# Layer 0's key and value evacuation: key low parts written by VectorE into the other partition half, values split in one operation per engine

## The chip, the cores and the metric

One core of a Trainium2 chip runs the whole program in one launch. The metric is the device time of one execution in microseconds (us). The engines are named as in the profile: PE (TensorE matmul), PEld (its weight load), DVE (VectorE), ACT (ScalarE), POOL (GpSimd) and SP (SyncE, which issues nearly all DMAs here; its queue is SPq).

## The reference, cut to what matters

The input is 512 tokens of 1024 features in float32. Layer 0 normalises x, multiplies by one wide matrix (`even_w_in`) and runs two groups of 16 attention heads of 64 channels on the result: forgetting attention ("F") and a mixture of dilated windows ("D"). Each has a gate path; the gated outputs go through `even_w_out` and are added to x. Layer 1 is a retention layer, which the change does not touch, and a last normalisation follows.

```python
def even_layer(x, g_norm, w_in, b_f, w_out):
    z = rms_norm(x, g_norm) @ w_in
    qa, ka, va, ga, fa, qb, kb, vb, gb = jnp.split(z, cuts, axis=-1)
    ...
    ya = forgetting_attention(hA(qa), hA(ka), hA(va), log_f).reshape(Bsz, S, WIDTH_FOX)
    yb = dilated_attention(hB(qb), hB(kb), hB(vb)).reshape(Bsz, S, WIDTH_DIL)
    y = jnp.concatenate([ya * jax.nn.silu(ga), yb * jax.nn.silu(gb)], axis=-1)
    return x + y @ w_out
```

## The kernel before

**Numbers as a sum of two.** Matmul operands are `F32R` values, which keep less of a float32 than it has. So each operand x is held as a high part, written by ACT as a copy into an `F32R` tile, and a low part, written by DVE as x minus the high part. The helper `split` (lines 138 to 144) does one such pair: ACT at L140, DVE at L142. A projection makes three matmuls per pair of operands (`three`, L199 to L201). All the split operations of the kernel have these two lines, so one tells them apart by the tile names: `w_h` and `w_l` are weights, `ka` and `kl` keys, `v` values, `pth` and `ptl` transposed probabilities, `yh` and `yl` gated outputs.

**Groups of heads.** Layer 0's 32 heads are worked in 8 groups of four heads (`ORDER = "DFFFFDDD"`). Each group has four projections of 256 columns: values (`proj_tokens`, result `pt`), keys and queries (`proj_features`, results `pf`, two blocks b of 128 channels, that is two heads each), and the gate. When the last matmul of a block is issued, its `done` function evacuates the PSUM bank: `evac_v`, `evac_k`, `evac_q`, `evac_gate`.

**Keys.** The score matmul of one head contracts over 128 rows: 64 channels of the key's high part and 64 of its low part in one tile, against a query tile arranged in the same way (L491, L492). So of one block, head 0 needs tile `ka` = [high of channels 0 to 63; low of channels 0 to 63] and head 1 needs `kb` = [low of channels 64 to 127; high of channels 64 to 127]. Before, `evac_k` split the whole block into `ka` (high) and a scratch tile `kl` (low), and three DMAs on the sync queue moved halves to the other partitions. `kl` has a single buffer, so the DVE subtraction of the second block waits until the first block's two transfers out of `kl` have landed. There are 16 key blocks: 8 groups of two.

**Values.** `evac_v` gets a bank with two token tiles of four heads of 64 channels. For an even head the value tile holds [high, low], for an odd head [low, high], side by side in 128 columns. Before, the even heads were split by one pair of operations and the odd heads by another, each of 256 elements a partition. There are 16 such banks too.

**The order of the work.** `interleave` runs the attention steps of one group and fills between them with the matmuls of the next group's projections and the output projection, by an estimated share of PE time. A step issues the scores of one head (`softmax_block`: scores, DVE maximum `pi` at L495, ACT exponential at L497, DVE reciprocal at L498, POOL scaling at L499), the transposes of the head before it (`transpose_block`, L506, split into `pth` and `ptl`) and its product with the values (`pv_block`, L518 with `pth`, L519 with `ptl`). `finish_head` adds the two halves of a finished head (`tmp` by ACT at L532, `y` by DVE at L533, both 64 partitions by 512), and every second head POOL multiplies the gate and a split makes `yh` and `yl`. Each engine runs its instructions in one order. Outside of a few marked sections that order is drawn up from the program's dependencies by a scheduler when the program is built.

**Buffers.** Projection results share three PSUM banks (tag `p`). Raw weights (`raw`), `wh` and `wl` have three buffers each. Key tiles have six buffers. Weights are loaded by SP (L164), and a load waits until the raw buffer three loads back has been split. SP's queue is in order: key transfers (L445 to L447), query transfers (L457 to L461), weight loads and the forget-gate rows (L545) stand in one line.

Of the kernel before, what the change touches and what calls it, by code (L numbers as in the profile page):

```python
# [9 lines left out]
F32R = mybir.dt.float32r  # L10
AF = mybir.ActivationFunctionType
ALU = mybir.AluOpType
PSUM = bass.MemoryType.PSUM

P = 128
S = 512
# [43 lines left out]
def trunk(ctx: ExitStack, tc, x, even_norm, even_w_in, even_b_f, even_w_out,  # L60
          odd_norm, odd_w_in, odd_w_out, final_norm, ident_d, dil_d, causal_d, rot_d, dec_d, out):
    nc = tc.nc
    pe, act, dve, pool = nc.tensor, nc.scalar, nc.vector, nc.gpsimd
    dma = nc.sync.dma_start
# [10 lines left out]
    def r32(ap):  # L75
        return ap.bitcast(F32)
# [61 lines left out]
    def split(hi, lo, src, scale=1.0):  # L138

        act.activation(hi, src, AF.Copy, scale=scale)  # L140
        if scale == 1.0:
            dve.tensor_tensor(lo, src, r32(hi), ALU.subtract)  # L142
        else:
            dve.scalar_tensor_tensor(lo, src, scale, r32(hi), ALU.mult, ALU.subtract)
# [206 lines left out]
    with ExitStack() as l0:  # L351
        cst = l0.enter_context(tc.tile_pool(name="cst0", bufs=1))
        qp = l0.enter_context(tc.tile_pool(name="qp", bufs=5))
# [83 lines left out]

        def evac_k(store):
            def done(b, ps):
                ka = qp.tile([P, S], F32R, tag="k", name="ka", bufs=6)  # L440
                kb = qp.tile([P, S], F32R, tag="k", name="kb", bufs=6)
                kl = qp.tile([P, S], F32R, tag="kl", name="kl", bufs=1)
                split(ka, kl, ps)

                dma(out=r32(kb[64:128, :]), in_=r32(kl[64:128, :]))  # L445
                dma(out=r32(kb[0:64, :]), in_=r32(ka[64:128, :]))
                dma(out=r32(ka[64:128, :]), in_=r32(kl[0:64, :]))  # L447
                store.extend([ka, kb])
            return done

# [14 lines left out]
        def evac_v(store):  # L465
            def done(b, ps):
                if b == 0:
                    store.append(gp.tile([P, NT, 4, P], F32R, tag="v", name="v"))
                src = ps.rearrange("p t (h d) -> p t h d", d=64)
                vv = store[0][:, 2 * b:2 * b + 2]  # L470

                split(vv[:, :, 0::2, 0:64], vv[:, :, 0::2, 64:128], src[:, :, 0::2, :])
                split(vv[:, :, 1::2, 64:128], vv[:, :, 1::2, 0:64], src[:, :, 1::2, :])
            return done

        def evac_gate(store):
# [388 lines left out]
```

## Time and profile before

| | |
|---|---|
| median of 3 runs | 1024.42 us (1022.52 to 1027.31) |
| the profiled execution's own time | 1027.15 us |
| its span | 1025.4 us |
| granted TensorE clock | 0.994 of full speed |
| PE busy | 995.8 us, 97% of the span |
| PEld busy | 841.4 us, 82% |
| DVE busy | 630.5 us, 61% |
| ACT busy | 473.6 us, 46% |
| POOL busy | 238.4 us, 23% |
| DMA | 106.82 MB, HBM read 84.87 MB |

The busy time of PE counts overlapping matmuls with a modelled end, so a gap of PE is best read from the start of one matmul to the start of the next. In rows of the timeline the first number is the start in us from the start of the span and the second the duration; brackets at the end give the idle time of that engine before the row and what ended it.

### The profile page before, as it was taken

The page shows a single profiled execution, that of the slowest core. Times are in us where ns is not written, and L with a number is a line of the kernel's source. Part 1 is how long each engine was busy: PE and PEld are TensorE (multiplying, and loading weights), DVE is VectorE, ACT ScalarE, POOL GpSimd, SP SyncE. Part 2 cuts the span into 40 slices and gives each one's busy share as a digit, 9 for nine tenths or more (in the row PEclk, how much of TensorE's full clock was granted, in tenths as well). Part 3 has the DMA queues.
Part 4 walks back from the last instruction along what each step waited for, and adds up shares of the span by engine and source line. Part 5 has one row for each costly group of instructions (what it writes and reads, how often), then busy time and mean ns, then how long its engine had stood idle before and what let it go on. Part 6 is the DMA issues. An engine that isn't in the chain of part 4 may idle for free.

```text
span 1025.4 us, 14433 instructions
## 1 busy us (share of the span) xinstructions
PE 995.8 (97%) x5170; PEld 841.4 (82%) x5170; DVE 630.5 (61%) x1382; ACT 473.6 (46%) x987; POOL 238.4 (23%) x340
## 2 busy tenths in 40 slices
PE   8999999999999999999999989999999999999997
PEld 6878888888887987988988769877888888888875
DVE  6365676575574675675657684377635844683476
ACT  6355464554544644645657464333323332333333
POOL 1011444444344442211212140023100300030012
PEclk9999999999999999999999999999999999999999
DMA  7664777645656775437444126222222232322112
GB/s 204 135 136 88 167 90 117 158 96 121 142 98 118 126 88 139 103 81 156 72 126 123 42 62 205 83 81 83 69 76 82 82 103 61 93 87 89 62 42 83
DMA packets 77130, 106.82 MB, mean 104 GB/s; under 512 B 6001, under 2 KB 49265, under 8 KB 76930
## 3 DMA queue, kind: packets, MB, share of 16 engines
q1 hardware_dynamic: 77058, 105.90, 43.8%
q8 instruction: 41, 0.67, 0.3%
q14 instruction: 31, 0.25, 0.1%
HBM read 84.87 MB, written 2.13 MB: 85 GB/s over the span
## 4 chain that ended last, share of the span: by engine, by line
PE 79%; DVE 8%; DMA 6%; ACT 4%; issue 2%; POOL 1%; SPq 0%; DVEq 0%; POOLq 0%; ACTq 0%
PE pf L199 10%; PE pf L200 10%; PE pf L201 10%; PE pw L201 5%; PE pw L200 5%; PE pw L199 5%; PE po L199 5%; PE po L201 4%; PE po L200 4%; PE pt L201 3%; PE pt L199 3%; PE pt L200 3%; PE ps_pt L506 3%; DVE w_l L142 2%; DMA kb<-ka 2%; PE ps_o L519 2%
## 5 line engine op out<-in xcount | busy, mean ns | idle before, releaser
L142 DVE TENSOR_TENSOR w_l<-w_raw,w_h 128x512 fp32r<-128x512 f32 x288 | 215.0, 773 | 103.0 <-ACT w_h L140 89.1
L140 ACT ACTIVATE w_h<-w_raw 128x512 fp32r<-128x512 f32 x288 | 169.7, 628 | 194.6 <-PE pf L200 61.8
L199 PE MATMUL pf<-xT,w_h 128*128 128x512 f32 x512 | 202.0, 394 | 0.0
L201 PE MATMUL pf<-xT,w_l 128*128 128x512 f32 x512 | 200.9, 392 | 0.0
L200 PE MATMUL pf<-xT,w_h 128*128 128x512 f32 x512 | 200.8, 392 | 0.0
L499 POOL TENSOR_SCALAR pi<-pi,st 128x512 f32<-128x512 f32 (+3 forms) x128 | 73.3, 574 | 374.1 <-DVE st L498 336.2
L201 PEld LDWEIGHTS pf<-xT,w_l 128*128 128x128 f32 x512 | 96.3, 188 | 21.2
L199 PEld LDWEIGHTS pf<-xT,w_h 128*128 128x128 f32 x512 | 96.6, 189 | 18.5
L200 PEld LDWEIGHTS pf<-xT,w_h 128*128 128x128 f32 x512 | 96.5, 188 | 18.2
L140 ACT ACTIVATE pth<-ps_pt 128x512 fp32r<-128x512 f32 (+3 forms) x128 | 55.3, 432 | 95.8 <-PE ps_pt L506 83.3
L497 ACT ACTIVATE pi<-pi,st 128x512 f32<-128x512 f32 (+3 forms) x128 | 71.5, 559 | 46.9 <-DVE st L495 46.2
L199 PE MATMUL pt<-w_h,xT 128*128 128x256 f32 x320 | 92.0, 288 | 1.1 <-ACT w_h L140 0.9
L201 PE MATMUL pt<-w_h,xT 128*128 128x256 f32 x320 | 91.2, 285 | 1.6 <-DVE xT L142 1.6
L200 PE MATMUL pt<-w_l,xT 128*128 128x256 f32 x320 | 91.2, 285 | 0.0
L199 PE MATMUL pw<-w_h,xT 128*128 128x512 f32 x224 | 88.4, 394 | 0.0
L201 PE MATMUL pw<-w_h,xT 128*128 128x512 f32 x224 | 87.8, 392 | 0.0
L200 PE MATMUL pw<-w_l,xT 128*128 128x512 f32 x224 | 87.7, 392 | 0.0
L778 POOL TENSOR_TENSOR yn<-yn,gate 128x512 f32<-128x512 f32 x16 | 21.0, 1312 | 265.2 <-DVE yn L777 265.2
L296 DVE TENSOR_TENSOR xres<-po,xres 128x512 f32<-128x512 f32 x88 | 59.6, 683 | 26.3 <-PE po L201 25.6
L142 DVE TENSOR_TENSOR ptl<-ps_pt,pth 128x512 fp32r<-128x512 f32 (+3 forms) x128 | 62.2, 487 | 20.8 <-ACT pth L140 19.1
L199 PEld LDWEIGHTS pt<-w_h,xT 128*128 128x128 f32 x320 | 61.5, 192 | 2.5 <-ACT w_h L140 1.3
L201 PEld LDWEIGHTS pt<-w_h,xT 128*128 128x128 f32 x320 | 61.4, 192 | 1.8 <-DVE xT L142 1.8
(176 smaller groups left out, 1882.8 us busy)
## 6 DMA issues: line engine op xcount, KB each, us to landing
w_raw<-in_even_w_in_dram SPq DMA_DIRECT2D x64, 512.0 KB, 5.8
w_raw<-in_odd_w_in_dram SPq DMA_DIRECT2D x48, 512.0 KB, 3.6
w_raw<-in_even_w_out_dram SPq DMA_DIRECT2D x16, 512.0 KB, 4.3
w_raw<-in_odd_w_out_dram SPq DMA_DIRECT2D x16, 512.0 KB, 3.6
qb<-qa SPq DMA_DIRECT2D x32, 128.0 KB, 2.8
qb<-qa SPq DMA_DIRECT2D x16, 256.0 KB, 3.0
qa<-qa SPq DMA_DIRECT2D x32, 128.0 KB, 2.8
cs<-c_dram SPq DMA_DIRECT2D x16, 256.0 KB, 3.7
```

The costliest lines, as they stand in the source:

```text
L140: act.activation(hi, src, AF.Copy, scale=scale)
L142: dve.tensor_tensor(lo, src, r32(hi), ALU.subtract)
L199: pe.matmul(ps, lhsT=ah, rhs=bh, start=first, stop=False)
L200: pe.matmul(ps, lhsT=ah, rhs=bl, start=False, stop=False)
L201: pe.matmul(ps, lhsT=al, rhs=bh, start=False, stop=last)
L296: dve.tensor_tensor(xr, ps, xr, ALU.add)
L497: act.activation(pi[:, 0:n], pi[:, 0:n], AF.Exp, bias=st[:, 0:1], scale=-1.0, accum_out=st[:, 1:2])
L499: pool.tensor_scalar(pi[:, 0:n], pi[:, 0:n], st[:, 2:3], 1.0, ALU.mult, ALU.mult)
L506: pe.transpose(pt[:, (i - j) * P:(i - j + 1) * P], hs["p"][i][:, j * P:(j + 1) * P], ident)
L519: pe.matmul(po[:, j * P:S], lhsT=v, rhs=tl[:, 0:n], start=False, stop=(j == NT - 1))
L778: pool.tensor_tensor(yn, yn, r["g"][:, i, :], ALU.mult)
```

## The change

`evac_k` no longer makes `kl` and issues no DMA. For each block it makes four operations on 64 partitions by 512: ACT copies channels 0 to 63 into the lower half of `ka`, DVE subtracts and writes the low part into the upper half of `ka`, ACT copies channels 64 to 127 into the upper half of `kb`, DVE writes their low part into the lower half of `kb`. DVE thus reads one half of the partitions and writes the other. `evac_v` makes the split of a bank in one ACT operation and one DVE operation of 512 elements a partition, by an access pattern that takes the blocks of 64 columns 0, 3 of each pair of heads for the high parts and 1, 2 for the low parts.

```diff
         def evac_k(store):
             def done(b, ps):
+
                 ka = qp.tile([P, S], F32R, tag="k", name="ka", bufs=6)
                 kb = qp.tile([P, S], F32R, tag="k", name="kb", bufs=6)
-                kl = qp.tile([P, S], F32R, tag="kl", name="kl", bufs=1)
-                split(ka, kl, ps)
-
-                dma(out=r32(kb[64:128, :]), in_=r32(kl[64:128, :]))
-                dma(out=r32(kb[0:64, :]), in_=r32(ka[64:128, :]))
-                dma(out=r32(ka[64:128, :]), in_=r32(kl[0:64, :]))
+                for k, own, other in ((ka, slice(0, 64), slice(64, 128)), (kb, slice(64, 128), slice(0, 64))):
+                    act.activation(k[own, :], ps[own, :], AF.Copy)
+                    dve.tensor_tensor(k[other, :], ps[own, :], r32(k[own, :]), ALU.subtract)
                 store.extend([ka, kb])
             return done
...
-                src = ps.rearrange("p t (h d) -> p t h d", d=64)
-                vv = store[0][:, 2 * b:2 * b + 2]
-
-                split(vv[:, :, 0::2, 0:64], vv[:, :, 0::2, 64:128], src[:, :, 0::2, :])
-                split(vv[:, :, 1::2, 64:128], vv[:, :, 1::2, 0:64], src[:, :, 1::2, :])
+
+                vv = store[0][:, 2 * b:2 * b + 2].rearrange("p t (h e) (c d) -> p (t h) (e c) d", e=2, c=2)
+                split(vv[:, :, 0::3], vv[:, :, 1:3], ps.rearrange("p t (h e d) -> p (t h) e d", e=2, d=64))
             return done
```

## The prediction

> **What bounds the kernel now.** I read the head of the page first, then the waits, then the chain that ended last around the longest of them, and last the timelines of PE, ACT and DVE at the evacuations. From the page, busy time by engine:
>
> ```profile
> PE 995.8 (97%) x5170; PEld 841.4 (82%) x5170; DVE 630.5 (61%) x1382; ACT 473.6 (46%) x987; POOL 238.4 (23%) x340
> ```
>
> PE is the bound, and no PE instruction is added or removed. So the change can only win back time in which PE stands still or runs slowly, and it can only lose by new stands. The waits name the places (who waited for whom: us in total, times, longest):
>
> ```profile
> SPq L447 <- DMA kb<-ka: 29.0, 10, 5.3
> DVE kl L142 <- DMA ka<-kl: 13.6, 6, 3.8
> PE ps_o L519 <- DVE ptl L142: 5.0, 4, 2.5
> PE po L199 <- DVE v L142: 2.0, 4, 0.5
> ```
>
> DVE stands for `kl` six times, PE stands four times for `ptl` and four times for `v`. The chain in order of time (start, duration, what) shows that the first two belong together:
>
> ```profile
> 311.68 0.61 ACT ka L140
> ...
> 312.30 7.04 DMA kb<-ka
> ...
> 319.37 2.17 DMA ka<-kl
> ...
> 321.66 0.69 DVE kl L142
> 322.35 0.59 DVE w_l L142
> 322.94 0.47 DVE pi L495
> ...
> 323.42 0.48 DVE ptl L142
> ```
>
> The first block's transfer took 7.04 us, SP issued the last transfer out of `kl` only then, DVE stood until it landed, and behind `kl` in DVE's queue stood `w_l`, `pi` and `ptl`, for which PE waits. That releaser is not only a name: 319.37 plus 2.17 is 321.54, and `kl` starts 0.12 later.
>
> **The change part by part. First what the key scratch costs PE.** Timeline of PE, the same pair of matmuls undisturbed, and at the longest stand, with what follows:
>
> ```profile
> 178.31 0.42 PE L518 MATMUL ps_o<-pth,v 128*128 128x384 f32 x1
> 178.57 0.34 PE L519 MATMUL ps_o<-ptl,v 128*128 128x384 f32 x1
> ...
> 321.00 0.42 PE L518 MATMUL ps_o<-pth,v 128*128 128x384 f32 x1
> 323.95 0.69 PE L519 MATMUL ps_o<-ptl,v 128*128 128x384 f32 x1 [2.52 <-DVE ptl L142]
> 324.43 0.63 PE L199 MATMUL pf<-xT,w_h 128*128 128x512 f32 x1
> ...
> 326.97 0.40 PE L199 MATMUL pf<-xT,w_h 128*128 128x512 f32 x1
> 327.20 0.40 PE L200 MATMUL pf<-xT,w_h 128*128 128x512 f32 x1
> ```
>
> Undisturbed the pair is 0.26 us apart, here 2.95: 2.69 lost, 0.17 more than the idle time shown, since a matmul's modelled end hides some. The four idles sum to 5.0 (the wait above), so the four stands cost about 5.0 + 4 x 0.16 = 5.6. After the longest, six matmuls from 324.43 to 326.97 take 2.54, against 6 x 0.23 = 1.38 at the pitch of the last two rows, and the `L519` before them 0.48 instead of 0.28: 1.36 more. Key term before: 5.6 + 1.4 = 7.0 us.
> The clock fell after a gap of 2.95 us. [...]
>
> **What replaces it.** Removed: 16 DVE and 16 ACT operations of 128x512, 48 transfers and their issues. Added: 32 and 32 of 64x512. The same view of single tiles gives durations (ns, least/median/most); half the partitions cost as much as all:
>
> ```profile
> L140 ACT ACTIVATE ka<-pf x16: 577/591/599, 38.1 to 521.8; 128x512 fp32r<-128x512 f32 x16
> L142 DVE TENSOR_TENSOR kl<-pf,ka x16: 685/692/693, 38.7 to 523.8; 128x512 fp32r<-128x512 f32 x16
> L532 ACT ACTIVATE tmp<-ps_o x32: 589/594/598, 84.7 to 588.9; 64x512 f32<-64x512 f32 x32
> L533 DVE TENSOR_TENSOR y<-ps_o,tmp x32: 671/688/696, 85.3 to 589.7; 64x512 f32<-64x512 f32 x32
> ```
>
> `tmp` already writes other partitions than it reads, at 594 ns. A DVE operation that does so is not in the trace; I take `y`'s 688. So each key block costs 0.59 of ACT and 0.69 of DVE more, 9.5 and 11.0 us in all. With ACT at 46% and DVE at 61% of the span the sum of busy time decides nothing; the order at the four stands does. How the four operations of a block overlap is unknown: ACT's second copy and DVE's first subtraction read different halves of one PSUM bank. The nearest rows are the old value evacuation, whose two pairs also read different parts of one bank (ACT and DVE timelines; then PE and the second bank):
>
> ```profile
> 142.69 0.36 ACT L140 ACTIVATE v<-pt 128x256 fp32r<-128x256 f32 x1
> 143.54 0.39 ACT L140 ACTIVATE v<-pt 128x256 fp32r<-128x256 f32 x1 [0.49 <-DVE v L142]
> ...
> 143.08 0.42 DVE L142 TENSOR_TENSOR v<-pt,v 128x256 fp32r<-128x256 f32 x1
> ...
> 145.66 0.42 DVE L142 TENSOR_TENSOR v<-pt,v 128x256 fp32r<-128x256 f32 x1
> 146.18 1.93 DVE L142 TENSOR_TENSOR w_l<-w_raw,w_h 128x512 fp32r<-128x512 f32 x2
> 148.03 0.41 DVE L142 TENSOR_TENSOR v<-pt,v 128x256 fp32r<-128x256 f32 x1
> ...
> 147.71 0.39 PE L201 MATMUL po<-w_h,yl 128*128 128x512 f32 x1
> 148.59 0.47 PE L199 MATMUL po<-w_h,yh 128*128 128x512 f32 x1 [0.49 <-DVE v L142]
> ```
>
> There ACT's second copy waits for DVE (0.49): ACT, DVE, ACT, DVE, one after the other. I take that order for the keys: 0.60 + 0.69 + 0.60 + 0.69 and three handovers of 0.04, 2.7 us from first to last. Now the stand near 250 us:
>
> ```profile
> 245.31 0.58 ACT L140 ACTIVATE ka<-pf 128x512 fp32r<-128x512 f32 x1
> ...
> 245.43 0.69 DVE L142 TENSOR_TENSOR yl<-y,yh 128x512 fp32r<-128x512 f32 x1 [0.15 <-ACT yh L140]
> 248.07 0.69 DVE L142 TENSOR_TENSOR kl<-pf,ka 128x512 fp32r<-128x512 f32 x1 [1.95 <-DMA ka<-kl]
> ...
> 249.09 0.42 PE L518 MATMUL ps_o<-pth,v 128*128 128x384 f32 x1
> 250.36 0.44 PE L519 MATMUL ps_o<-ptl,v 128*128 128x384 f32 x1 [0.85 <-DVE ptl L142]
> ```
>
> Serial: DVE is free of `yl` at 246.12; first subtraction 246.15 to 246.84; ACT 246.88 to 247.48; second subtraction to 248.20; then as in the chain `w_l` 0.60, `pi` 0.48, `ptl` 0.55, done at 249.86. PE would issue L519 at 249.09 + 0.26 = 249.35, so a stand of about 0.55 stays. In four places that is 2.2, and none is long enough to cost clock. If the halves overlap, ACT is done by 246.5, DVE does both at 246.15 and 246.87, `ptl` is done by 249.25 and the stand is nil. If ACT idles in the chain for the first block too, everything behind it (`pth`, `tmp`, `y`, `yh`, `yl`) slides by about 1.3 and the stand grows to 1.9. So the new key term is 2.2, bounds 0 and 4 x 1.9 = 7.6.
> A detail on DVE's side, after an operation on half the partitions:
>
> ```profile
> 525.13 0.69 DVE L533 TENSOR_TENSOR y<-ps_o,tmp 64x512 f32<-64x512 f32 x1
> 525.85 0.56 DVE L495 CUSTOM_DVE_ANT_0 pi<-ps_s,dil 128x384 f32<-128x384 f32 x1
> ```
>
> The next one starts 0.72 after it, where in the chain above `w_l` to `pi` is 0.59. [...]
>
> **Values.** Four operations of 0.36 and 0.42 become two of 0.59 and 0.69 (as `ka` and `kl`, also 512 elements): ACT 0.13 and DVE 0.15 less per bank, 2 us each in all, off the path. What counts is the second subtraction: at 148.03 it stands behind two `w_l`, and PE's next output tile waits for its bank: 148.59 less 147.71 is 0.88, 0.23 undisturbed, 0.65 lost, four times 2.6. With one pair the only subtraction stands where the first one stood (145.66), runs to about 146.6 and frees the bank 1.3 before PE asks. `w_l` slides to about 148.4 and the first `po` sum behind it to 149.1, before the fourth tile needs that bank at 147.94 plus six matmuls of 0.23, 149.3. Value term: 2.6 to zero; bounds 0 (if the one subtraction goes behind `w_l`) and 2.9 (with the slow restart of 0.08 each).
>
> **The sync queue.** The 48 issues and the 29.0 us of waiting inside SP's line go. Weight loads behind them mostly wait for `w_l` anyway, so I give nothing there, except in the first group, where the query transfers compete with late loads and PE waits for a query half:
>
> ```profile
> 58.07 0.39 PE L200 MATMUL pf<-xT,w_h 128*128 128x512 f32 x1
> 58.64 0.68 PE L491 MATMUL ps_s<-ka,qa 128*128 128x512 f32 x2 [0.17 <-DMA qa<-qa]
> ```
>
> 0.57 instead of 0.23: 0.3 to win, bounds 0 and 0.3.
>
> **The sum.** 1027.15 (the profiled execution's own time) less 7.0 plus 2.2, less 2.6, less 0.3: **1019.4**. That execution is 2.7 above the median of the runs, 1024.42; its longest key wait with the slow clock (2.69 + 1.36) could be that difference, but no second trace is there to say so. Against the median the forecast is 5.0 less.
>
> **The rivals.**
> 1. *The halves overlap, or the scheduler fills the waits.* For it: ACT and DVE touch different partitions, unlike the value pairs. Against: the value rows wait although they touch different columns. Key term 7.0 to zero: 1027.15 - 7.0 - 2.6 - 0.3 = 1017.2, 1016.9 with the value bound.
> 2. *The stall only changes its name.* The serial chain also delays the first block, the stand is 1.9 at each of four places: 1027.15 - 7.0 + 7.6 - 2.9 = 1024.9, about the median. For it: the 0.49 that ACT idled in the value rows. Against: it stacks every delay in full, and the first block's copy starts 12 us before the late `ptl` in the chain (311.68 to 323.42), of which 9 were transfers (7.04 and 2.17) that go. The same time comes out if `kl` was not what held DVE (the rows above speak against it) or the order is drawn up unluckily elsewhere.
> 3. *Slower.* The four operations, in both in-order queues, push `ptl` so late that the gaps reach the 2.95 that cost clock before. Place: the L519 after the second key block. Each such stand costs 2.7 + 1.4 = 4.1; four cost 16.4: 1027.15 - 7.0 + 16.4 - 2.9 = 1033.6. It decides for slower (over 1029.5) from a mean cost of 3.1 per place. Against: even the late case above gives 1.9.
>
> **How the numbers follow.** 0.5% of the median, 5.1 us, is about what a measurement of this kernel can tell. Chances: forecast 0.40 (about half of it below 1019.3), rival 1 0.32, rival 2 0.20, rival 3 0.08. Faster 0.20 + 0.32 = 0.52; same 0.20 + 0.20 = 0.40; slower 0.08. The range takes rival 1 with two us for an order drawn up anew, 1014.5, and rival 2, 1025.0; rival 3 and some tails stay out. The likeliest's own range is 1017.5 to 1021.5.
>
> **What would show it.** No wait of DVE for a transfer before a key subtraction; `ps_o L519 <- ptl` down from 5.0 to about 1.5 idle, or to nil for rival 1; no `po L199 <- v`; no dip of the clock near 320 us; ACT up 7 us, DVE 9, PE busy unchanged; key subtractions at about 0.69 with starts 0.72 apart. The prediction is wrong if the DVE write to other partitions takes much over 0.69, if key subtractions queue so that L519 waits longer than 1, or if the value subtraction still stands behind `w_l`.

## The result, and the profile after

The changed kernel takes 1018.88 us (median of 5 runs, 1016.67 to 1019.48) beside 1026.6 us of the kernel before in the same comparison (5 runs): a ratio of 0.993, 95% interval 0.992 to 0.995. The profiled execution took 1019.2 us, with a span of 1017.2. The forecast was 1019.4. Lines up to 443 and names are as before; the key copies are L444, the key subtractions L445, and everything behind them has a number lower by four (`ps_o<-ptl` is L515, the scores L487 and L488).

From the page, busy time by engine, and then what PE waited for among the groups of heads (us in total, times, longest); its other waits above half a microsecond lie at the start, in the forget gates, at the end of layer 0 and in layer 1:

```profile
PE 992.6 (98%) x5170; PEld 840.3 (83%) x5170; DVE 637.0 (63%) x1382; ACT 481.6 (47%) x987; POOL 240.0 (24%) x340
```

```profile
PE ps_o L515 <- DVE ptl L142: 1.7, 5, 0.4
PE ps_o L514 <- ACT pth L140: 1.1, 2, 0.6
PE ps_s L487 <- DMA qa<-qa: 0.2, 1, 0.2
```

The 5.0 us of idle time for `ptl` are 1.7, the line `po L199 <- v` is gone, and no wait of DVE for a transfer stands before a key subtraction. One of the two waits for `pth` is new, 0.62 at 518 us: the kernel with new keys alone has it too, the one with new values alone has not. The place of the old 2.95 us gap, in the timeline of PE:

```profile
317.91 0.42 PE L514 MATMUL ps_o<-pth,v 128*128 128x384 f32 x1
318.69 0.45 PE L515 MATMUL ps_o<-ptl,v 128*128 128x384 f32 x1 [0.35 <-DVE ptl L142]
318.97 0.39 PE L199 MATMUL pf<-xT,w_h 128*128 128x512 f32 x1
319.20 0.40 PE L200 MATMUL pf<-xT,w_h 128*128 128x512 f32 x1
```

The pair is 0.78 apart, 0.52 more than undisturbed, and the next matmuls follow at 0.23: the clock does not fall. Five such stands are left, at 177, 248, 319, 389 and 460 us, about 0.5 each and 2.5 together. How one of them comes about is seen 70 us earlier, on ACT and DVE:

```profile
244.20 0.63 ACT L140 ACTIVATE yh<-y 128x512 fp32r<-128x512 f32 x1 [1.44 <-POOL y L531]
...
245.38 0.59 ACT L444 ACTIVATE kb<-pf 64x512 fp32r<-64x512 f32 x1
...
243.05 0.69 DVE L445 TENSOR_TENSOR ka<-pf,ka 64x512 fp32r<-64x512 f32 x1
244.87 0.76 DVE L142 TENSOR_TENSOR yl<-y,yh 128x512 fp32r<-128x512 f32 x1 [1.13 <-ACT yh L140]
245.54 0.68 DVE L142 TENSOR_TENSOR w_l<-w_raw,w_h 128x512 fp32r<-128x512 f32 x1
246.25 0.69 DVE L445 TENSOR_TENSOR kb<-pf,kb 64x512 fp32r<-64x512 f32 x1
246.98 0.56 DVE L491 CUSTOM_DVE_ANT_0 pi<-ps_s,bias 128x384 f32<-128x384 f32 x1
...
247.46 0.55 DVE L142 TENSOR_TENSOR ptl<-ps_pt,pth 128x384 fp32r<-128x384 f32 x1
```

The first subtraction is done early. The second is not: its copy stands on ACT behind `yh`, which waits for POOL's `y`. From `yl` on DVE runs without a pause, `yl`, `w_l`, `kb`, `pi`, `ptl`, and PE waits for the end of that row. So no transfer sets these places now, but the row on DVE and, ahead of it, the end of `y` on POOL.

### The profile page after: what moved, and what is told of

It is laid out like the page before. It is cut to its first block, busy times and chain, and to the rows that moved or that the text cites. A ratio compares the mean times of both kernels' runs of the same rounds, so it can differ in the third digit from the quotient of the medians.

```text
span 1017.2 us, 14317 instructions
## 1 busy us (share of the span) xinstructions
PE 992.6 (98%) x5170; PEld 840.3 (83%) x5170; DVE 637.0 (63%) x1382; ACT 481.6 (47%) x987; POOL 240.0 (24%) x340
## 4 chain that ended last, share of the span: by engine, by line
PE 86%; DVE 7%; ACT 2%; DMA 2%; issue 2%; POOL 1%; DVEq 0%; POOLq 0%; ACTq 0%; SPq 0%
PE pf L199 10%; PE pf L200 10%; PE pf L201 10%; PE pw L200 5%; PE pw L201 5%; PE pw L199 5%; PE po L199 5%; PE po L201 5%; PE po L200 5%; PE pt L201 3%; PE pt L199 3%; PE pt L200 3%; PE ps_pt L502 3%; PE ps_o L515 2%; PE ps_o L514 2%; PE ps_s L488 2%
## 5 line engine op out<-in xcount | busy, mean ns | idle before, releaser
L142 DVE TENSOR_TENSOR w_l<-w_raw,w_h 128x512 fp32r<-128x512 f32 x288 | 210.7, 758 | 97.7 <-ACT w_h L140 83.9
L199 PE MATMUL pf<-xT,w_h 128*128 128x512 f32 x512 | 201.5, 394 | 0.0
L199 PEld LDWEIGHTS pf<-xT,w_h 128*128 128x128 f32 x512 | 96.2, 188 | 18.3
L199 PE MATMUL pt<-w_h,xT 128*128 128x256 f32 x320 | 91.4, 286 | 0.1
L199 PE MATMUL pw<-w_h,xT 128*128 128x512 f32 x224 | 88.4, 395 | 0.0
L199 PEld LDWEIGHTS pt<-w_h,xT 128*128 128x128 f32 x320 | 61.1, 191 | 1.1 <-ACT xT L140 0.6
```

The costliest lines, as they stand in the source:

```text
L199: pe.matmul(ps, lhsT=ah, rhs=bh, start=first, stop=False)
```

## The experiments

All times are against the kernel before, run on the same chip in the same comparison; its medians there were 1024.55, 1024.7 and 1024.78.

**Each part alone.** The first run has the new `evac_k` with the old `evac_v`:

```diff
-                vv = store[0][:, 2 * b:2 * b + 2].rearrange(...)
-                split(vv[:, :, 0::3], vv[:, :, 1:3], ps.rearrange(...))
+                split(vv[:, :, 0::2, 0:64], vv[:, :, 0::2, 64:128], src[:, :, 0::2, :])
+                split(vv[:, :, 1::2, 64:128], vv[:, :, 1::2, 0:64], src[:, :, 1::2, :])
```

> The changed key evacuation, the old value evacuation. Theory (two separate gains, both from waits of PE): the four stands of PE for the second value subtraction come back, 2.6 us, so about 1021.5, ratio to the kernel before 0.995; in its trace PE stands four times about 0.5 us for v. Rival (the two parts share one gain, or the value part only shifted the order): as the changed kernel, 1018.9.

Measured: 1019.41 us, ratio 0.995 [0.993, 0.996]. The second has the old `evac_k` with the new `evac_v` (the same lines the other way round).

> The old key evacuation with scratch and transfers, the changed value evacuation. Theory: the value stands go (2.6 us less than the kernel before, 1024.0, ratio 0.9975), and the stands of PE for ptl behind the key scratch stay, with the clock dip where a stand is near 3 us. Rival (all of the gain is the keys'): 1026.6, ratio 1.0.

Measured: 1020.59 us, ratio 0.996 [0.995, 0.998]. The changed kernel once more, as a mark for the second series:

> The changed kernel once more, as the measure for the three others beside it on the same chip. Both theories: ratio 0.993, five stands of PE of about 0.35 for ptl.

Measured: 1018.6 us, ratio 0.994 [0.993, 0.996].

Alone the parts bring 5.1 and 4.0 us, together 6.1. (The 7.7 of the first comparison rest on 5 runs of the kernel before, these 6.1 on 23.) They are not additive, and the waits show where. PE's waits with new keys alone, and then with new values alone:

```profile
PE ps_o L517 <- DVE ptl L142: 1.7, 5, 0.4
PE po L199 <- DVE v L142: 0.7, 4, 0.2
```

```profile
PE ps_o L517 <- DVE ptl L142: 2.9, 2, 2.4
PE ps_s L489 <- DMA qa<-qa: 1.0, 1, 1.0
```

With new keys alone the value wait, which the prediction had given to the values, falls from 2.0 to 0.7 by itself, as it does in the next run, which has the old values and two `kl` buffers. With new values alone the key wait falls from four stands (5.0) to two (2.9), though `kl` still waits 11.3 us for its transfers. It seems that a shift of a few tenths in a row of in-order queues decides whether PE sees a late operation; which shift does it was not followed. So either part alone brings most of the 6 us.

**Wait or transfers?** Two `kl` buffers in the kernel before, which end DVE's wait but keep all 48 transfers (room came from two small tiles of the forget gates; that move was not run alone, but PE's waits show no new row for it):

```diff
-                kl = qp.tile([P, S], F32R, tag="kl", name="kl", bufs=1)
+                kl = qp.tile([P, S], F32R, tag="kl", name="kl", bufs=2)
```

> The kernel before with two buffers for the scratch tile kl; to make room, two small tiles of the forget gates are put into buffers that are idle then. All 48 transfers stay, and neither ACT nor DVE gets more work. Theory (the single scratch buffer was the wait, not the traffic or the sync queue): DVE no longer stands for a transfer, the whole key term of 7.0 us goes, with no stand left over: 1019.6, ratio 0.993, and no wait of PE for ptl over 0.3. Rival (the transfers themselves cost, through the sync queue or the DMA engines): less than 3 us gained, 1024 or more.

Measured: 1024.61 us, ratio 1.000 [0.999, 1.001]. The theory was wrong, and by a way that neither side had named. The waits of PE have no `ptl` any more, but this:

```profile
PE ps_s L491 <- DMA qa<-qa: 4.9, 2, 3.2
```

The chain that ended last before the longer of the two (start, duration, what):

```profile
326.10 0.70 DVE qa L144
...
326.82 8.28 DMA qb<-qa
...
335.16 2.19 DMA qa<-qa
...
337.48 0.64 PE ps_s L491 x2
```

A query transfer of 256 KB takes 8.28 us; the next one overwrites what it reads and waits for it, and the first score waits for that. It was near before: there, in the second group, the transfer that the first score waits for was issued at 118.68, and the score started at 121.48, 2.8 later, where such a transfer takes 2.2 at least. The reverse was then made: the changed kernel, with no `kl` and no wait, and 48 useless transfers of 128 KB behind the key blocks (results unused; the same two small tiles moved):

```diff
+                kx = qp.tile([P, S], F32R, tag="kx", name="kx", bufs=1)
+                dma(out=r32(kx[64:128, :]), in_=r32(kb[64:128, :]))
+                dma(out=r32(kx[0:64, :]), in_=r32(ka[0:64, :]))
+                ky = qp.tile([P, S], F32R, tag="ky", name="ky", bufs=1)
+                dma(out=r32(ky[0:64, :]), in_=r32(kb[64:128, :]))
```

> The changed kernel with 48 transfers of 128 KB put back, three behind each key block, from the finished key tiles into two scratch tiles that nothing reads; two small forget-gate tiles are moved into buffers idle then, to make room. No engine waits for them; what is measured is the sync queue and the DMA engines alone. Theory (the transfers make the query transfers and the weight loads late, as in the kernel with two scratch buffers, where PE came to stand 4.9 us for qa): PE stands for qa again, 2 to 5 us more than the changed kernel, ratio 0.995 to 0.998. Rival (traffic is free, and the kernel with two scratch buffers lost its gain only by the order of its instructions): as the changed kernel, 0.993.

Measured: 1024.08 us, ratio 0.999 [0.998, 1.000]: transfers for which no engine waits take back nearly all of the gain. Whether it is their issue or their bytes, this run does not say. PE's wait for query halves:

```profile
PE ps_s L492 <- DMA qa<-qa: 3.3, 2, 3.1
```

Then both at once, two `kl` buffers and a query evacuation with one transfer fewer, which writes each half's own part directly:

```diff
-                split(qa[:, 0, :], qa[:, 1, :], ps, scale=-0.125)
...
+                for q, own, other in ((qa, slice(0, 64), slice(64, 128)), (qb, slice(64, 128), slice(0, 64))):
+                    split(q[own, 0, :], q[own, 1, :], ps[own, :], scale=-0.125)
+                    dma(out=r32(q[other, 1, :]), in_=r32(q[own, 0, :]))
+                    dma(out=r32(q[other, 0, :]), in_=r32(q[own, 1, :]))
```

> The kernel with two scratch buffers, with the query evacuation changed: both query tiles get their own halves directly by ACT and DVE (64x512 each, twice as many operations) and only the other halves by transfers, so that no query transfer waits for another; 64 transfers instead of 80. Theory (with two scratch buffers the key stand went, and the query transfers, which wait for one another, took its place): the stands for qa go, and the gain comes out: 1018 to 1020, ratio 0.994 to 0.996. Rival (the key transfers cost by themselves, or DVE's added work eats it): 1023 or more, ratio over 0.998.

Measured: 1037.29 us, ratio 1.012 [1.010, 1.014]; the theory was wrong. PE's order came out differently: the planner puts the first scores of a group ahead of projection matmuls that had stood before them, and PE meets them too early, with a stand of 5.2 for a query half and another of 4.9 that the trace puts down to issue. It says nothing about the transfers.

Is it SP's queue or the bytes? Two `kl` buffers again, with the key transfers issued by POOL, and the same with the new values:

```diff
-                dma(out=r32(kb[64:128, :]), in_=r32(kl[64:128, :]))
+                nc.gpsimd.dma_start(out=r32(kb[64:128, :]), in_=r32(kl[64:128, :]))
...
```

> The kernel before with two `kl` buffers, and the 48 key transfers issued by POOL instead of SP; the values as before. With two buffers and SP, PE stood 1.65 and 3.23 us for query halves, and the slow clock came behind the second (together about 5 us). Theory Q: the query transfers were late because they queue in SP behind key transfers and weight loads that wait. Then they start early here, the two stands of PE for `qa` are together under 1 us, and the ratio is about 0.995 (1019 to 1020.5 us). Theory E: the 48 transfers take the 16 DMA engines while weight loads and query halves need them, whoever issues them. Then a stand of 2 to 3 us for `qa` stays, and the ratio is 0.998 to 1.000. Rival P: POOL, in order, holds `y` back behind a wait for `kl`; then `yh` and `ptl` come late, with stands for `ptl` near 1 us and a ratio above 0.998.

> As the run with two `kl` buffers and POOL's queue, with the new values (one pair of operations). The value stands there were 0.16 us each, so both theories expect at most 0.7 us less than that run. If theory Q holds, this keeps every transfer and comes to 1018.5 to 1020 us, the time of the changed kernel: then it is the wait and the queue that cost, not the bytes. If theory E holds, 1022 to 1024.

Measured: 1038.37 us, ratio 1.013 [1.011, 1.016], and 1035.48 us, 1.011 [1.008, 1.013]. As versions both are bad, and they leave the question open. Waits of the first, one of POOL and two of PE:

```profile
POOL ka L447 <- DMA kb<-ka: 48.2, 15, 6.1
...
PE ps_pt L506 <- POOL pi L499: 10.9, 4, 4.4
PE ps_s L491 <- DMA qa<-qa: 0.5, 1, 0.5
```

The wait for query halves falls from 4.9 to 0.5 (and to 0.8 in the second) with all 48 transfers kept. But PE itself comes late: its two longest stands for `pi`, 114.48 to 119.28 and 335.31 to 339.75 from start to start, lie shortly before the scores at which it had stood with SP's queue. From the issue of the first query transfer to the first score it takes 13.9 and 10.5 us there, against 8.0 in the changed kernel; late queries would hardly have been seen. What is left as evidence is the landing: the transfer that waits for the first 256 KB is issued 5.7 and 5.2 us after them, instead of 6.7 and 8.3. What was lost is rival P, at another tile than it named: POOL in order stands 48.2 us before the issues of the last transfer (L447), and behind them stands `pi`, the scaled probabilities, for which PE waits. In SP's queue the delay can be followed at the last projection weights before the queries of the second group, the issue by SP beside the `w_l` of DVE that frees the buffer. In the changed kernel, then with two `kl` buffers on SP, then on POOL:

```profile
103.75 0.96 DVE L142 TENSOR_TENSOR w_l<-w_raw,w_h 128x512 fp32r<-128x512 f32 x1
104.74 0.37 SPq L164 DMA_DIRECT2D w_raw<-in_even_w_in_dram  x1
112.56 0.47 SPq L457 DMA_DIRECT2D qb<-qa  x1
```

```profile
103.90 1.06 DVE L142 TENSOR_TENSOR w_l<-w_raw,w_h 128x512 fp32r<-128x512 f32 x1
105.35 0.54 SPq L445 DMA_DIRECT2D kb<-kl  x1
106.42 0.37 SPq L164 DMA_DIRECT2D w_raw<-in_even_w_in_dram  x1
112.85 0.47 SPq L459 DMA_DIRECT2D qb<-qa  x1
```

```profile
103.83 0.68 DVE L142 TENSOR_TENSOR w_l<-w_raw,w_h 128x512 fp32r<-128x512 f32 x1
104.54 0.37 SPq L164 DMA_DIRECT2D w_raw<-in_even_w_in_dram  x1
```

The buffer is free at 104.71, 104.96 and 104.51; the load is issued 0.03, 1.46 and 0.03 later. In the middle one it stands behind key transfers in SP's queue, and so comes 1.4 us nearer to the query transfers. (In the kernel before, DVE's wait for `kl` holds that key transfer back: it is issued at 107.40, behind the load at 105.71.)

That the later load makes the queries late was not tested alone, but kernels without any key transfer speak for a part of it. In the changed kernel the load is issued 7.8 us ahead of these queries, and the transfer that waits for the first 256 KB is issued 3.7 us after them. In the three kernels of the next part the load is issued 6.1 to 6.2 ahead, that time is 5.6 to 7.3, and PE stands 0.4 to 2.1 us. With key transfers and the load 7.7 to 7.8 ahead it is 4.5 (before) and 6.1 (new values alone). (In all of these a load of output weights goes out in between, 1.5 to 1.8 ahead of the queries.) So late loads and key transfers both go with late queries; how they share the DMA engines was not measured.

**What replaces the wait.** Both copies of a block, then both subtractions, so that no ACT operation waits for DVE:

```diff
                 for k, own, other in halves:
                     act.activation(k[own, :], ps[own, :], AF.Copy)
+                for k, own, other in halves:
                     dve.tensor_tensor(k[other, :], ps[own, :], r32(k[own, :]), ALU.subtract)
```

> The changed kernel with both ACT copies of a block ahead of both subtractions. Theory (in the changed kernel the second copy waits for the first subtraction and goes behind pth in ACT's order, and so the second subtraction comes late and leaves PE a stand of about 0.5 us in five places): the handover ACT, DVE, ACT, DVE becomes two by two, ptl lands 0.3 to 0.5 earlier, 1.5 to 2.5 us less than the changed kernel: 1016.4 to 1017.4, ratio 0.991. Rival (what remains is DVE's added 0.72 per block, whatever the order): no difference, 1018.9, ratio 0.993.

Measured: 1024.72 us, ratio 1.000 [0.999, 1.002]; the theory was wrong. (`halves` holds the two triples of the loop before.) DVE at the second place:

```profile
247.16 0.77 DVE L142 TENSOR_TENSOR yl<-y,yh 128x512 fp32r<-128x512 f32 x1 [1.25 <-ACT yh L140]
247.94 0.69 DVE L447 TENSOR_TENSOR ka<-pf,ka 64x512 fp32r<-64x512 f32 x1
248.64 0.69 DVE L447 TENSOR_TENSOR kb<-pf,kb 64x512 fp32r<-64x512 f32 x1
```

Now both subtractions come behind `yl`; the five stands are 0.67 to 0.75 of idle time each instead of 0.29 to 0.35. That is 2.0 of the 6 us. PE also stands 0.94 and 0.68 us for query halves, though this kernel has no key transfers; the rest was not followed. The serial order, which the expectation held to be a cost, let one subtraction go early. Two more runs put one DVE operation more into each key block: a useless subtraction of 64x512, and the copy into `kb` by DVE instead of ACT.

```diff
+                kx = qp.tile([P, S], F32R, tag="kx", name="kx", bufs=1)
+                for _ in range(1):
+                    dve.tensor_tensor(kx[0:64, :], ps[64:128, :], r32(kb[64:128, :]), ALU.subtract)
```

> The changed kernel with one more DVE subtraction of 64x512 behind each key block, into a tile that nothing reads: DVE's part of the price, dosed. Theory (PE's remaining stand is the end of DVE's in-order row behind the key block, so what is added there is paid in full at the five stands and nowhere else): ptl lands about 0.6 later, five stands of about 0.95 instead of 0.35, 3 us more than the changed kernel, ratio 0.996. Rival (DVE's added work is covered, and the stands have another cause): within 1 us of the changed kernel, ratio 0.993 to 0.994.

```diff
-                    act.activation(k[own, :], ps[own, :], AF.Copy)
+                    act.activation(k[own, :], ps[own, :], AF.Copy) if k is ka else dve.tensor_copy(k[own, :], ps[own, :])
```

> The changed kernel with the second high copy of a key block (into `kb`) made by DVE instead of ACT, so that no copy waits behind `yh` and `w_h` on ACT. DVE gains 16 x 0.7 = 11 us, ACT loses 9.5. Theory (the five stands of 0.51 us come from what DVE has to do after `yh`: `yl`, the second key subtraction and `w_l`, 2.1 us ahead of `pi` and `ptl`): the second subtraction still goes behind `yl`, so the stands stay at 0.3 to 0.5 and the time at 1018 to 1020 (ratio to the kernel before 0.994 to 0.996). Rival (the stands come from ACT's second copy standing behind `yh` and `w_h`): the stands go, 2 us less, ratio 0.992.

Measured: 1026.02 us, ratio 1.002 [1.000, 1.003], and 1026.13 us, 1.002 [1.000, 1.004]. The stand at the same matmul as above, with the start of `y` on DVE and of the pair's first matmul on PE, in the first and in the second:

```profile
317.65 0.69 DVE L532 TENSOR_TENSOR y<-ps_o,tmp 64x512 f32<-64x512 f32 x1
...
322.77 0.42 PE L517 MATMUL ps_o<-pth,v 128*128 128x384 f32 x1
324.34 0.44 PE L518 MATMUL ps_o<-ptl,v 128*128 128x384 f32 x1 [1.15 <-DVE ptl L142]
```

```profile
318.15 0.69 DVE L529 TENSOR_TENSOR y<-ps_o,tmp 64x512 f32<-64x512 f32 x1
...
323.29 0.42 PE L514 MATMUL ps_o<-pth,v 128*128 128x384 f32 x1
324.72 0.44 PE L515 MATMUL ps_o<-ptl,v 128*128 128x384 f32 x1 [1.02 <-DVE ptl L142]
```

0.35 becomes 1.15 and 1.02: 0.8 and 0.67 for one operation of 0.68 to 0.69. At these places DVE's time goes to PE about one to one, in six places, though DVE is busy 63% of the span. The way is another than the two expectations name, DVE's row behind the key block or behind `yh`. From the start of `yl` to the end of `ptl` that row takes 3.15 us in the changed kernel, and 3.37 and 3.23 here. Most of the time is lost further back: `y` starts 5.70 us before the pair's first matmul in the changed kernel (312.21 and 317.91) and only 5.12 and 5.14 before it here, because the added operation of the first key block stands ahead of it on DVE. From `y` to `yl`, through POOL and ACT, it is 3.27 to 3.28 us in all three.

The rival of the second run, that ACT's copy behind `yh` makes the stand, fell: without that copy the stands grew. Both runs cost more than the 3 us and the nothing that were expected; in the second the later `w_l` also frees the weight buffer later, at 107.50 instead of 104.71, and the query transfers are late again: PE stands 2.8 us for them, in two places. (In the first the load goes out later still, at 108.64, and PE waits only 0.4 for queries; so the load's time is not the whole rule.)

## Why the prediction was right, point by point

- **Key term, 7.0 before.** Right in kind: the key scratch held DVE, and DVE held PE. The 1.4 us of slow clock went with the gap. It was not as separable as the working had it: with new values alone 2 of the 4 stands go without any change to the keys.
- **Key term, 2.2 after.** Measured 2.5, in five stands of about 0.5 instead of four of 0.55. The serial order is in the trace where nothing else stands between (the first block, at 37.95 to 40.60 us, 2.65 in all, forecast 2.7):

```profile
39.29 0.59 ACT L444 ACTIVATE kb<-pf 64x512 fp32r<-64x512 f32 x1 [0.75 <-DVE ka L445]
39.91 0.69 DVE L445 TENSOR_TENSOR kb<-pf,kb 64x512 fp32r<-64x512 f32 x1 [0.66 <-ACT kb L444]
```

  At the stands it is not the handover that costs. The forecast had the first subtraction behind `yl` and an idle DVE while ACT copies; in fact that subtraction goes before `yl`, `w_l` fills the copy's time, and no DVE idle time is left. The two errors cancel, so that 2.2 came so near to 2.5 is luck. The run with both copies first, in which the first subtraction does go behind `yl`, has up to 0.75 of idle time at a stand where the changed kernel has 0.35. The stand of 0.62 for `pth` that came with the new keys is in no term.
- **Durations.** The trace bears out the price taken from `y` (0.688): a subtraction that writes the other half of the partitions takes what `y` took (median in ns in the middle of the three):

```profile
L445 DVE TENSOR_TENSOR ka<-pf,ka x16: 684/685/685, 38.6 to 514.5; 64x512 fp32r<-64x512 f32 x16
L445 DVE TENSOR_TENSOR kb<-pf,kb x16: 692/693/694, 39.9 to 516.5; 64x512 fp32r<-64x512 f32 x16
```

  The starts 0.72 apart came too: in the rows above `kb` starts 0.71 after `w_l`, and `pi` 0.73 after `kb`, where `yl` to `w_l` is 0.67. What makes the difference was not shown. ACT rose by 8.0 (forecast 7). DVE rose by 6.5, forecast 9: the keys' 11 and the values' 2.4 came as said, but the `w_l` group fell by 4.3, from 215.0 to 210.7 busy; the 2.1 that are left over were not traced. PE's busy time fell by 3.2, forecast unchanged; some of it is the slow clock's longer matmuls (six of 0.57 to 0.63 instead of 0.40 behind the old gap of 2.95).
- **Value term, 2.6.** The mechanism stood: one subtraction, where the first one stood, ahead of the two `w_l`, and no `po L199 <- v` left:

```profile
144.56 0.69 DVE L142 TENSOR_TENSOR v<-pt,v 128x512 fp32r<-128x512 f32 x1 [0.32 <-ACT v L140]
145.17 1.64 DVE L142 TENSOR_TENSOR w_l<-w_raw,w_h 128x512 fp32r<-128x512 f32 x2
```

  But 1.3 of the 2.0 us of idle time went without it, with new keys alone, so it is not the price of this edit alone.
- **First-group query wait, 0.3.** Gone: the first scores start 0.23 behind the matmul ahead of them, at 58.14 after 57.91. A wait of 0.24 for a query half stands at 474 us instead.
- **The sum, 1019.4.** Its terms come to a gain of 7.7, and in the two profiled executions the first transposes of layer 1 start at 601.74 and 594.34, 7.4 apart. But the terms were taken off an execution that was 2.7 above the median. Between medians of more runs the gain is 6.1, and the same terms off the median 1024.42 give 1016.7. So that the time came within 1 us of 1018.88 and 1018.6 is owed in part to the start of the sum. (The range's lower end, 1014.5, is 0.4 below 1016.9 less the two us that it names.)
- **The sync queue, nothing.** In the sum this held: PE waits 0.2 us for query halves before and after. As an account it failed. It looked at the queue for what waits in it now, and the queries waited little. It missed what the wait that the change removes had covered: take the wait alone and the queries take its place (two buffers, 1.000); take the transfers too and the gain is kept. The sum is right because the change took both, which the prediction did not argue: that is luck. Whether the queue or the bytes make the queries late stays open.
- **Rivals.** The halves did not overlap in the first block (rival 1); its other half, that the scheduler fills the waits, did come at the stands, but 0.5 us stayed at each of five. Rival 2, the stall that only changes its name, did not happen to this change but did happen to its neighbours: to `qa` with two buffers, and to later `ptl` with both copies first. No gap reached the one that rival 3 needs.

## What to carry to other kernels

When a wait is to be removed, ask what stands next behind it, in time and not only in the same queue, and price that too: here a version that removed only the wait won nothing (two `kl` buffers, ratio 1.000). Where a bound engine waits for the end of a row of operations on another, the row's work in that window can count in full, whatever that engine's share of the span: here one DVE operation of 0.68 to 0.69 more cost PE 0.8 and 0.67 at a stand, with DVE busy 63% of the span. The row begins further back than its last stretch without a pause: here an operation ahead of `y` reached PE through POOL and ACT, 3.27 to 3.28 us from `y` to `yl`. An operation that could go ahead of the row was worth more here than one handover fewer (ratio 0.994, against 1.000 with both copies first). Two edits that both shift the same in-order queues should be timed alone and together before each is given its share.

## What the runs showed of the hardware

Gaps of PE, from start to start, and the pitch of the 128x512 matmuls behind them. In layer 0, behind the start, four gaps were each followed by six or more matmuls at 0.43 instead of 0.23: 2.82 (new values alone, at 320.80), 2.95 (before), 3.49 and 3.62 (useless transfers, two buffers). Shorter ones went either way: 2.46 (the changed query evacuation, at 54.69) was followed by eight of them; 2.04 (two `kl` buffers, at 122.65) and 2.52 (the copy by DVE, at 123.99) by none. One place of layer 1 has it twice before the same instruction, in the changed kernel with a gap of 2.66 and with new keys alone with 2.65:

```profile
700.18 0.50 PE L199 MATMUL ps_r<-vh,ah 128*128 128x512 f32 x1 [2.28 <-DVE yn L773]
...
702.19 0.63 PE L201 MATMUL pw<-w_h,xT 128*128 128x512 f32 x1
702.62 0.63 PE L199 MATMUL pw<-w_h,xT 128*128 128x512 f32 x1
```

```profile
702.63 0.50 PE L199 MATMUL ps_r<-vh,ah 128*128 128x512 f32 x1 [2.26 <-DVE yn L775]
...
704.35 0.39 PE L201 MATMUL pw<-w_h,xT 128*128 128x512 f32 x1
704.57 0.39 PE L199 MATMUL pw<-w_h,xT 128*128 128x512 f32 x1
```

In the first seven matmuls go at 0.43, which costs some 1.4 us; in the second none does. Even two gaps of 1.9 us, 3 us apart at the start of layer 1, were followed by 128x256 matmuls at 0.21 in the kernel before (from 609.10) and at 0.12 in the changed one (from 600.64). The prediction has its stands of 0.55 as too short to cost clock, and behind the five of about 0.5 in the changed kernel the matmuls do follow at 0.23 to 0.24; but a gap of 2.95 is not needed for it. A stand of some 2.5 us could here cost about half as much again and need not; its length alone did not decide, and what else did, these rows do not show.

A transfer within SBUF of 128 or 256 KB landed after 2.2 us at least and 8.3 at most in the same kernel (two `kl` buffers). In the kernel before, two key transfers of 128 KB, one behind the other, took 7.04 and 2.17. What a transfer cost here is not read from its size alone.
